# Block sums of the Strassen-like feed-forward: two of four by accumulating transfers, signs moved to the tokens' sums, output chunks placed at bank copies

## The chip, the cores and the metric

The kernel runs on one core of a Trainium2 chip, which has five engines that run side by side: TensorE (PE, matrix products), VectorE (DVE), ScalarE (ACT), GpSimd (POOL) and SyncE (SP, which here only issues transfers). The metric is the device time of one execution in microseconds (us). Lower is better.

## The reference

One decoder layer on 256 tokens of width 1024: a mixing stage with two branches, attention over 256 memory tokens, and a gated feed-forward, each added to the residual stream, and a final norm. The change touches the feed-forward alone:

```python
hn = rmsnorm(h, norm_ffn_g[l])
gu = hn @ w_ffn_in[l]                       # (256, 1024) @ (1024, 5632)
h = h + (jax.nn.silu(gu[..., :FFN_HIDDEN]) * gu[..., FFN_HIDDEN:]) @ w_ffn_out[l]   # FFN_HIDDEN = 2816
return rmsnorm(h, final_norm_g)
```

All inputs and outputs are float32.

## The kernel before

**Products in three.** Each float32 operand is split into a high part (`hi`, rounded to the matmul's float32r) and a low part (`lo`, what is left), and each product is made of three matmuls: hi·hi, hi·lo and lo·hi. For a weight block of 128 x 2048, `halve` makes the high part on ScalarE (L1098) and the low part on VectorE (L1099). Every block of weights passes through these two lines once. Three `hi`/`lo` buffers rotate, with a fourth pair, `px`, for every fourth unit.

**Units of the feed-forward.** The hidden width of 2816 falls into 11 chunks of 256. The plan `FFN_PLAN` is a list of 42 units that TensorE runs in the order written:

- `("I", o, kh)`: the product of the tokens with one half (512 rows) of the input weights of chunk `o`, gate and value columns side by side. Ten of these units, for chunks 0, 1, 4, 7 and 10, are computed directly.
- `("P", q, name)`: chunks 2 and 3, 5 and 6, 8 and 9 are computed in pairs, three double groups `q` = 2, 5, 8. The two halves of the tokens (`t`), the two halves of the depth and the two chunks form a 2 x 2 by 2 x 2 block product, made with seven products instead of eight, in the order P1, P2, P6, P7, P5, P3, P4. Each is 12 matmuls of 512 columns.
- `("O", o)`: output chunk `o`, the product of the hidden values of chunk `o` with its output weights, accumulated in four PSUM banks (`acc`).

**Block sums.** `load_blocks(q)` loads four blocks of the group, named "22", "12", "11" and "21", from SyncE's queue (L1113). The seven products need four sums of these blocks, each made in place by `both` as two VectorE instructions of 128 x 1024 (L1106): one at the load (onto "12"), one for P6 (onto "11"), one for P5 (onto "12" again), one for P4 (onto "21"). The corresponding sums of the tokens (`token_sums`, L1241) are made once and split into `SS`.

**Banks.** P1, P6, P5 and P3 accumulate one after the other in bank A; P2 has bank B, P7 and P4 bank F. What bank A holds after P1, P6 and P5 is copied away by ScalarE (`keep`, L1275) before the next of them may write there. `whole` (L1280) adds a kept copy to another bank. When a half of the hidden values of a chunk is complete, `gate` makes the Silu on ScalarE (`fg`, L1205) and the product on VectorE (`fu`, L1208).

**Turns.** Before output chunk `o` can run, its hidden values are transposed on TensorE (`turn_hid`, L1210, four transposes into `hidT`) and split into `hids` (L310 on ScalarE, L311 on VectorE). `TURNS` says ahead of which unit this is done, and `LOADS` ahead of which unit the blocks of a group are asked for. Weights are prepared three units ahead (`prep_u(n + 3)`).

**Who sets the order.** TensorE's order is the program's. ScalarE, VectorE, GpSimd and SyncE are put in order by the framework's scheduler, by priority in program order and by what it estimates to be ready.

**A path not taken.** The kernel has an option `BY_DMA`, off, in which two of the four sums are made by accumulating transfers from GpSimd's queue, with a negated copy on ScalarE ahead of each (`less`, L1119).

Of the kernel before, what the change touches and what calls it, by code (L numbers as in the profile page):

```python
# [13 lines left out]
AF = mybir.ActivationFunctionType  # L14
ALU = mybir.AluOpType
# [58 lines left out]
def ffn_plan():  # L74
    def seven(q, **after):
        out = []
        for p in SEVEN:
            out.append(("P", q, p))
            out += [("O", o) for o in after.get(p, ())]
        return out  # L80

    def two(j):
        return [("I", j, 0), ("I", j, 1)]

    out = two(0) + two(1)
    out += seven(2, P2=[0], P5=[1]) + two(4)
    out += seven(5, P2=[2], P7=[3], P5=[4]) + two(7)
    out += seven(8, P2=[5], P7=[6], P5=[7])
    out += two(10) + [("O", 8)]
    return out + [("O", 9), ("O", 10)]  # L90

FFN_PLAN = ffn_plan()
BY_DMA = False
LOADS = {0: (2,), 10: (5,), 22: (8,)}
TURNS = {4: (0,), 8: (1,), 15: (2,), 18: (3,), 20: (4,), 27: (5,), 30: (6,), 32: (7,), 38: (8, 9)}


def lay(ws):
# [45 lines left out]
def build(tc, A, out):  # L144
    nc = tc.nc
    V, SC, G, PE, SY = nc.vector, nc.scalar, nc.gpsimd, nc.tensor, nc.sync
    with ExitStack() as ctx:
# [11 lines left out]
        def big(tag, name, shape=(128, 8, 256), dt=F32):  # L159
            return bp.tile(list(shape), dt, name=name, tag=tag)  # L160
# [69 lines left out]
        def nxt(lead=LEAD):  # L230
            i = at[0]
            at[0] += 1
            while made[0] <= min(i + lead, len(ORDER) - 1):
                run(prep())
            return ready.pop(i)
# [31 lines left out]
        def by_k(w, k):  # L267
            return tuple(t.rearrange("p (k c) -> p k c", k=k) for t in w)
# [265 lines left out]
        for i in range(9):  # L534
            if i < 8:
                c, k = i // 4, i % 4
# [4 lines left out]
            if i > 0:  # L541
                c, k = (i - 1) // 4, (i - 1) % 4
                for t in range(2):
                    PE.matmul(pss[c][t], Xh[:, k, t * 128:(t + 1) * 128], ws[c][1][:, k], start=False, stop=False)
        w = by_k(nxt(), 4)
# [15 lines left out]
        w = by_k(nxt(), 4)  # L561
# [483 lines left out]
        for c in range(4):  # L1045
            gemm_f(H1, ev_sum(qxh, qxl, c))
            g = scores(c)
# [36 lines left out]
        where = {u: i for i, u in enumerate(ORDER)}  # L1084
        px = big("P1", "px", (128, 4096), F32R)
        made_u, pair, blk = [0], {}, {}

        def halve(raw, n):
            if n % 4 == 3:
                hi, lo = px[:, 0:2048], px[:, 2048:4096]  # L1090
            else:
                hi = wh.tile([128, 2048], F32R, name="hi", tag="hi")
                lo = wl.tile([128, 2048], F32R, name="lo", tag="lo")
            pieces = 2 if n < 2 else 1
            w = 2048 // pieces
            for c in range(pieces):
                a = slice(c * w, (c + 1) * w)
                SC.activation(hi[:, a], raw[:, a], AF.Copy)  # L1098
                V.tensor_tensor(lo[:, a], raw[:, a], hi[:, a].bitcast(F32), op=ALU.subtract)  # L1099
            return hi, lo  # L1100


        def both(out, x, y, op):
            for i in range(2):
                a = slice(1024 * i, 1024 * i + 1024)
                V.tensor_tensor(out[:, a], x[:, a], y[:, a], op=op)  # L1106

        def load_blocks(q):
            blk.clear()
            for key, tag, c in (("22", "B12", (q + 1, 1)), ("12", "B6", (q + 1, 0)),  # L1110
                                ("11", "B10", (q, 0)), ("21", "B11", (q, 1))):
                blk[key] = big(tag, "b" + key, (128, 2048))
                SY.dma_start(blk[key], A["w"][where[("I",) + c]])  # L1113
            if BY_DMA:
                less(blk["12"], blk["12"], (q + 1, 1))
            else:
                both(blk["12"], blk["22"], blk["12"], ALU.subtract)

        def less(out, x, c):  # L1119
            SC.activation(out, x, AF.Copy, scale=-1.0)  # L1120
            G.dma_start(out, A["w"][where[("I",) + c]], accum_op=ALU.add)

        def block(q, name):
            if name == "P7" and BY_DMA:
                less(blk["21"], blk["11"], (q, 1))
            if name == "P6":
                both(blk["11"], blk["12"], blk["11"], ALU.add)
            elif name == "P5":
                both(blk["12"], blk["22"], blk["11"], ALU.subtract)
            elif name == "P4" and not BY_DMA:  # L1130
                both(blk["21"], blk["21"], blk["11"], ALU.subtract)
            return blk[{"P1": "11", "P2": "21", "P6": "11", "P7": "12", "P5": "12", "P3": "22", "P4": "21"}[name]]

        units = FFN_PLAN
# [50 lines left out]
        for t in range(2):  # L1185
            for c in range(2):
                ps = mm.tile([128, 512], F32, name="pso", tag="mm")
# [11 lines left out]
        X2 = (h2h, h2l)  # L1199
        hid, acc, psi, hm = {}, {}, {}, {}  # L1200

        def gate(o, t):
            ps = psi.pop((o, t))
            g = t2b("fg", (128, 256))
            SC.activation(g, ps[:, 0:256], AF.Silu)  # L1205
            if o not in hm:
                hm[o] = t2("fu", (128, 2, 256))
            V.tensor_tensor(hm[o][:, t], ps[:, 256:512], g, op=ALU.mult)  # L1208

        def turn_hid(o):  # L1210
            bk = mm.tile([128, 2, 256], F32, name="hidT", tag="mm")
            u = hm.pop(o)
            for t in range(2):
                for j in range(2):
                    PE.transpose(bk[:, j, t * 128:(t + 1) * 128], u[:, t, j * 128:(j + 1) * 128], ident)
            hd = hids[o // 2 % 2][:, o % 2]
            split(bk, hd[:, 0], hd[:, 1])
            hid[o] = hd

        def out_part(o, w, t, c, home=None, u=0, v=512):  # L1220
            if home is None and (t, c) not in acc:
                acc[t, c] = bank("acc")
            ps = home or acc[t, c]
            ts, cs = slice(t * 128, (t + 1) * 128), slice(c * 512 + u, c * 512 + v)
            for k in range(2):
                hh, hl = hid[o][:, 0, k], hid[o][:, 1, k]
                mm3t(ps, hh[:, ts], hl[:, ts], w[0][:, k, cs], w[1][:, k, cs],
                     (o == 0 or home is not None) and k == 0, k == 1 and o >= NF // 2 - (2 if t and c else 1))
# [12 lines left out]
        def token_sums():  # L1241
            a11, a12, a21, a22 = (h2g[t, c] for t in range(2) for c in range(2))

            def put(i, g):
                SC.activation(SS[:, 0, i], g, AF.Copy)
                V.tensor_tensor(SS[:, 1, i], g, SS[:, 0, i].bitcast(F32), op=ALU.subtract)

            V.tensor_tensor(a22, a21, a22, op=ALU.add)
            s2 = t2("s2", (128, 4, 128))
            V.tensor_tensor(s2, a22, a11, op=ALU.subtract)  # L1250
            put(1, s2)
            V.tensor_tensor(a21, a11, a21, op=ALU.subtract)
            put(2, a21)
            put(0, a22)
            V.tensor_tensor(a12, a12, s2, op=ALU.subtract)
            put(3, a12)

        def tokens(name):
# [13 lines left out]
        bank_of, kept = {}, {}  # L1272
# [4 lines left out]

        def whole(q, t, ps, key):
            c = t2("fc")
            V.tensor_tensor(c, ps, kept.pop(key), op=ALU.add)  # L1280
            psi[q, t] = c
            gate(q, t)

        def ffn_product(n):
            _, q, name = units[n]
            w = by_k(pair[n], 4)
            key = {"P1": "A", "P6": "A", "P5": "A", "P3": "A", "P2": "B", "P7": "F", "P4": "F"}[name]
            first = name in ("P1", "P2", "P7")
            if first:
                bank_of[key] = mm.tile([128, 512], F32, name="pq" + key, tag="mm")  # L1290
            ps = bank_of[key]
            product(ps, name, w, first)
            if name == "P1":
                keep("1", ps, t2("f1"))
            elif name == "P2":
                whole(q, 0, ps, "1")
            elif name == "P6":
                keep("2", ps, gf[:, 1024:1536])
            elif name == "P5":
                keep("4", ps, gf[:, 1536:2048])  # L1300
                whole(q + 1, 1, bank_of["F"], "4")
            elif name == "P3":
                psi[q + 1, 0] = ps
                gate(q + 1, 0)
            elif name == "P4":
                whole(q, 1, ps, "2")

        def ffn_out(n):
            w = by_k(pair[n], 2)
            for t in range(2):  # L1310
                for c in range(2):
                    out_part(units[n][1], w, t, c)


        prep_u(3)
# [11 lines left out]
        for n in range(4, len(units) - 2):  # L1327
            for q in LOADS.get(n, ()):
                load_blocks(q)
            prep_u(n + 3)  # L1330
            for o in TURNS.get(n, ()):
                turn_hid(o)
# [11 lines left out]
        n = NF // 2 - 1  # L1344
# [38 lines left out]
        with tc.manual_schedule(engines={E.Activation, E.DVE, E.Pool, E.SP}):  # L1383
# [24 lines left out]
            for i in range(2):  # L1408
                a = slice(512 + 256 * i, 768 + 256 * i)
# [46 lines left out]
```

## Time and profile before

| | |
|---|---|
| time, median of 3 runs | 620.22 us (620.06 to 620.54) |
| profiled execution | 619.96 us, span 618.2 us |
| granted TensorE clock | 0.999 |
| the feed-forward's products | from about 430 us to 610 us of the span |
| transfers, feed-forward blocks | `b<-w` 12 of 1024 KB, median 5.9 us from issue to landing |

All times of rows are microseconds from the start of the span. A row of the order of time has its start, its duration, the engine, the line, the operation, what it writes and reads, and in square brackets the engine's idle time just before it and what ended that. Adjacent rows of an engine overlap a little, since an instruction's start and end are in the pipeline of the next one. In a table by stage, each engine has its busy time in the stretch and the number of its instructions. A group's row ends with its busy time, the mean of one in ns, and the idle time of its engine just before these instructions.

### The profile page before, as it was taken

How to read it: one execution, taken by the hardware profiler on the slowest of the kernel's cores; microseconds unless marked ns; L12 is line 12 of the kernel's file. 1: busy time of each engine (PE TensorE's matmuls, PEld its weight loads, DVE VectorE, ACT ScalarE, POOL GpSimd, SP SyncE). 2: the span in 40 equal slices, each digit the busy share in tenths (PEclk: the TensorE clock that was granted, in tenths of full speed). 3: DMA queues.
4: the chain of work that ended last, by engine and by line, in shares of the span. 5: the costliest groups of instructions: out<-in, count | busy, mean ns of one | idle time of the engine just before them, and what ended most of it. 6: DMA issues, size and time to landing. Idle time of an engine off the chain costs nothing.

```text
span 618.2 us, 8376 instructions
## 1 busy us (share of the span) xinstructions
PE 607.5 (98%) x3117; PEld 506.7 (82%) x3117; DVE 460.0 (74%) x714; ACT 355.2 (57%) x545; POOL 256.5 (41%) x227
## 2 busy tenths in 40 slices
PE   8999999999999999999999999999998999999995
PEld 7888888888877877778888888888886888888884
DVE  7589988979766875747855456655799897997743
ACT  7785554334376756736456566746567556565432
POOL 3888744556544464355876876720000000000003
PEclk9999999999999999999999999999999999999999
DMA  8753553334543333644454554463815718613311
GB/s 346 289 204 150 205 200 140 137 136 140 189 150 136 137 137 124 208 181 149 191 205 152 193 200 156 163 227 142 335 68 193 283 69 325 218 68 137 141 64 68
DMA packets 16888, 107.50 MB, mean 174 GB/s; under 512 B 2000, under 2 KB 2640, under 8 KB 4560
## 3 DMA queue, kind: packets, MB, share of 16 engines
q1 hardware_dynamic: 16128, 106.14, 46.5%
q10 hardware_dynamic: 720, 0.84, 0.4%
q8 instruction: 24, 0.39, 0.2%
q14 instruction: 16, 0.13, 0.1%
HBM read 105.92 MB, written 1.05 MB: 173 GB/s over the span
## 4 chain that ended last, share of the span: by engine, by line
PE 89%; DVE 7%; issue 1%; ACT 1%; DMA 1%; POOL 0%; POOLq 0%; DVEq 0%; ACTq 0%
PE pst L263 13%; PE pst L265 13%; PE pst L264 13%; PE psf L284 7%; PE pqA L1269 4%; PE psf L285 4%; PE acc L265 3%; PE acc L263 3%; PE acc L264 3%; DVE lo L1099 2%; PE psi L263 2%; PE psi L265 2%; PE pqF L1269 2%; PE psi L264 2%; PE lp L638 2%; DVE b L1106 1%
## 5 line engine op out<-in xcount | busy, mean ns | idle before, releaser
L223 POOL TENSOR_TENSOR lo<-raw,hi 128x448 fp32r<-128x448 f32 x106 | 161.7, 1540 | 110.6 <-ACT hi L219 107.8
L219 ACT ACTIVATE hi<-raw 128x1024 fp32r<-128x1024 f32 (+1 forms) x128 | 128.7, 1028 | 93.7 <-PE pst L265 58.1
L223 DVE TENSOR_TENSOR lo<-raw,hi 128x576 fp32r<-128x576 f32 (+2 forms) x128 | 131.1, 1031 | 57.2 <-ACT hi L219 54.2
L263 PE MATMUL pst<-hi,XX 128*128 128x512 f32 x224 | 90.5, 404 | 0.0
L265 PE MATMUL pst<-hi,XX 128*128 128x512 f32 x224 | 87.4, 390 | 0.0
L264 PE MATMUL pst<-lo,XX 128*128 128x512 f32 x224 | 87.4, 390 | 0.0
L1374 POOL TENSOR_TENSOR hg<-H,gf 128x512 f32<-128x512 f32 x3 | 3.8, 1290 | 172.1 <-DVE H L1366 172.1
L1099 DVE TENSOR_TENSOR lo<-raw,hi 128x2048 fp32r<-128x2048 f32 (+1 forms) x21 | 43.7, 2086 | 12.2 <-ACT hi L1098 12.1
L265 PEld LDWEIGHTS pst<-hi,XX 128*128 128x128 f32 x224 | 42.1, 188 | 9.0
L263 PEld LDWEIGHTS pst<-hi,XX 128*128 128x128 f32 x224 | 42.1, 188 | 8.8 <-issue 0.7
L264 PEld LDWEIGHTS pst<-lo,XX 128*128 128x128 f32 x224 | 42.2, 188 | 7.8
L1098 ACT ACTIVATE hi<-raw 128x2048 fp32r<-128x2048 f32 (+1 forms) x21 | 36.6, 1750 | 16.4 <-issue 5.6
L1099 DVE TENSOR_TENSOR lo<-b,hi 128x2048 fp32r<-128x2048 f32 x13 | 29.8, 2289 | 8.0 <-ACT hi L1098 8.0
L265 PE MATMUL acc<-hi,hids 128*128 128x512 f32 x78 | 30.7, 393 | 1.7 <-DVE hids L311 1.7
L1098 ACT ACTIVATE hi<-b 128x2048 fp32r<-128x2048 f32 x13 | 24.9, 1914 | 12.1 <-PE acc L265 6.2
L263 PE MATMUL acc<-hi,hids 128*128 128x512 f32 x78 | 30.7, 393 | 0.0
L264 PE MATMUL acc<-lo,hids 128*128 128x512 f32 x78 | 30.4, 390 | 0.0
L1106 DVE TENSOR_TENSOR b<-b,b 128x1024 f32<-128x1024 f32 x24 | 28.5, 1219 | 0.0
L263 PE MATMUL psi<-hi,H 128*128 128x512 f32 x72 | 28.1, 391 | 0.0
L265 PE MATMUL psi<-hi,H 128*128 128x512 f32 x72 | 28.1, 390 | 0.0
L264 PE MATMUL psi<-lo,H 128*128 128x512 f32 x72 | 28.0, 389 | 0.0
L284 PE MATMUL psf<-H,hi 128*128 128x512 f32 x64 | 22.8, 400 | 0.0
(402 smaller groups left out, 1485.1 us busy)
## 6 DMA issues: line engine op xcount, KB each, us to landing
raw<-w SPq DMA_DIRECT2D x82, 1024.0 KB, 4.8
b<-w SPq DMA_DIRECT2D x12, 1024.0 KB, 5.9
raw<-w SPq DMA_DIRECT2D x4, 512.0 KB, 6.3
raw<-w SPq DMA_DIRECT2D x4, 256.0 KB, 4.0
H<-xtok SPq DMA_DIRECT2D x1, 1024.0 KB, 9.5
mraw<-mT SPq DMA_DIRECT2D x1, 1024.0 KB, 4.8
xraw<-xT SPq DMA_DIRECT2D x1, 512.0 KB, 6.4
gf<-gfin SPq DMA_DIRECT2D x1, 512.0 KB, 3.6
```

What stands on the lines that cost most here:

```text
L219: SC.activation(hi[:, a], raw[:, a], AF.Copy)
L223: eng.tensor_tensor(lo[:, b], raw[:, b], hi[:, b].bitcast(F32), op=ALU.subtract)
L263: PE.matmul(ps, xh, h, start=first, stop=False)
L264: PE.matmul(ps, xh, l, start=False, stop=False)
L265: PE.matmul(ps, xl, h, start=False, stop=last)
L284: PE.matmul(ps, w[0][:, k, a], X2[:, :, k], start=k == 0, stop=False)
L285: PE.matmul(ps[:, 0], w[1][:, k, a], X2[:, 0, k], start=False, stop=k == 7)
L638: PE.matmul(ps[:, j], KS[:, a0 + j], QQ[:, a0 + j], start=True, stop=True)
L1098: SC.activation(hi[:, a], raw[:, a], AF.Copy)
L1099: V.tensor_tensor(lo[:, a], raw[:, a], hi[:, a].bitcast(F32), op=ALU.subtract)
L1106: V.tensor_tensor(out[:, a], x[:, a], y[:, a], op=op)
L1269: PE.matmul(ps, x[k], z[:, k], start=first and k == 0 and i == 0, stop=k == 3 and i == 2, skip_group_check=not first)
```

## The change

Two of the four block sums of each double group are taken from VectorE: the one at the load becomes a transfer from memory that adds onto block "12", and the one for P4 becomes a transfer inside the core's memory that adds block "11" onto block "21". Both are issued by GpSimd. A transfer can only add, so the block product is written with other signs: the two chunks of a group trade places (`q` and `q + 1`), the signs of the tokens' sums, of P3's gate and of the sum that uses P5's copy change, and the subtractions of blocks that are made by transfer become additions.

Beside it, three smaller things. The high part of every unit is made in two ScalarE instructions of 128 x 1024 (before, only for the first two units), while the low part stays one instruction. In the first double group output chunk 0 moves from behind P2 to behind P7. The turns move to earlier units: those of chunks 2, 5 and 8 now stand right behind P4, ahead of the next direct unit. `MIDWAY` is empty and does nothing.

```diff
-    out = two(0) + two(1)
-    out += seven(2, P2=[0], P5=[1]) + two(4)
+    out = two(0) + two(1) + seven(2, P7=[0], P5=[1]) + two(4)
...
-BY_DMA = False
+BY_DMA = (2, 5, 8)
 LOADS = {0: (2,), 10: (5,), 22: (8,)}
-TURNS = {4: (0,), 8: (1,), 15: (2,), 18: (3,), 20: (4,), 27: (5,), 30: (6,), 32: (7,), 38: (8, 9)}
+TURNS = {4: (0,), 6: (1,), 13: (2,), 16: (3,), 18: (4,), 25: (5,), 28: (6,), 30: (7,), 37: (8,), 38: (9,)}
...
+            for c in range(2):
+                a = slice(c * 1024, (c + 1) * 1024)
+                SC.activation(hi[:, a], raw[:, a], AF.Copy)
             pieces = 2 if n < 2 else 1
             w = 2048 // pieces
             for c in range(pieces):
                 a = slice(c * w, (c + 1) * w)
-                SC.activation(hi[:, a], raw[:, a], AF.Copy)
                 V.tensor_tensor(lo[:, a], raw[:, a], hi[:, a].bitcast(F32), op=ALU.subtract)
...
-            for key, tag, c in (("22", "B12", (q + 1, 1)), ("12", "B6", (q + 1, 0)),
-                                ("11", "B10", (q, 0)), ("21", "B11", (q, 1))):
+            for key, tag, c in (("22", "B12", (q, 1)), ("12", "B6", (q, 0)),
+                                ("11", "B10", (q + 1, 0)), ("21", "B11", (q + 1, 1))):
...
-            if BY_DMA:
-                less(blk["12"], blk["12"], (q + 1, 1))
+            if q in BY_DMA:
+                G.dma_start(blk["12"], A["w"][where["I", q, 1]], accum_op=ALU.add)
             else:
-                both(blk["12"], blk["22"], blk["12"], ALU.subtract)
+                both(blk["12"], blk["22"], blk["12"], ALU.add)
...
             if name == "P6":
                 both(blk["11"], blk["12"], blk["11"], ALU.add)
+            elif name == "P7" and q in BY_DMA:
+                G.dma_start(blk["21"], blk["11"], accum_op=ALU.add)
             elif name == "P5":
-                both(blk["12"], blk["22"], blk["11"], ALU.subtract)
-            elif name == "P4" and not BY_DMA:
-                both(blk["21"], blk["21"], blk["11"], ALU.subtract)
+                both(blk["12"], blk["11"], blk["22"], ALU.subtract)
+            elif name == "P4" and q not in BY_DMA:
+                both(blk["21"], blk["21"], blk["11"], ALU.add)
...
-        def gate(o, t):
+        def gate(o, t, sign=1.0):
...
-            SC.activation(g, ps[:, 0:256], AF.Silu)
+            SC.activation(g, ps[:, 0:256], AF.Silu, scale=sign)
...
+            if sign < 0:
+                V.scalar_tensor_tensor(hm[o][:, t], ps[:, 256:512], sign, g, op0=ALU.mult, op1=ALU.mult)
...
-            V.tensor_tensor(a22, a21, a22, op=ALU.add)
+            V.tensor_tensor(a22, a22, a21, op=ALU.subtract)
             s2 = t2("s2", (128, 4, 128))
-            V.tensor_tensor(s2, a22, a11, op=ALU.subtract)
+            V.scalar_tensor_tensor(s2, a22, -1.0, a11, op0=ALU.mult, op1=ALU.subtract)
...
-            V.tensor_tensor(a12, a12, s2, op=ALU.subtract)
+            V.scalar_tensor_tensor(a12, s2, -1.0, a12, op0=ALU.mult, op1=ALU.subtract)
...
             elif name == "P2":
-                whole(q, 0, ps, "1")
+                whole(q + 1, 0, ps, "1")
...
             elif name == "P5":
                 keep("4", ps, gf[:, 1536:2048])
-                whole(q + 1, 1, bank_of["F"], "4")
+                whole(q, 1, bank_of["F"], "4")
             elif name == "P3":
-                psi[q + 1, 0] = ps
-                gate(q + 1, 0)
+                psi[q, 0] = ps
+                gate(q, 0, -1.0)
             elif name == "P4":
-                whole(q, 1, ps, "2")
+                whole(q + 1, 1, ps, "2")
```

More of the change, by code (lines that the diff above doesn't have):

```diff
@@ L92 @@
 FFN_PLAN = ffn_plan()
-BY_DMA = False
+BY_DMA = (2, 5, 8)
 LOADS = {0: (2,), 10: (5,), 22: (8,)}
-TURNS = {4: (0,), 8: (1,), 15: (2,), 18: (3,), 20: (4,), 27: (5,), 30: (6,), 32: (7,), 38: (8, 9)}
+TURNS = {4: (0,), 6: (1,), 13: (2,), 16: (3,), 18: (4,), 25: (5,), 28: (6,), 30: (7,), 37: (8,), 38: (9,)}
+MIDWAY = {}
 def lay(ws):
@@ L1109, in load_blocks @@
             blk.clear()
-            for key, tag, c in (("22", "B12", (q + 1, 1)), ("12", "B6", (q + 1, 0)),
-                                ("11", "B10", (q, 0)), ("21", "B11", (q, 1))):
+            for key, tag, c in (("22", "B12", (q, 1)), ("12", "B6", (q, 0)),
+                                ("11", "B10", (q + 1, 0)), ("21", "B11", (q + 1, 1))):
                 blk[key] = big(tag, "b" + key, (128, 2048))
                 SY.dma_start(blk[key], A["w"][where[("I",) + c]])
-            if BY_DMA:
-                less(blk["12"], blk["12"], (q + 1, 1))
-            else:
-                both(blk["12"], blk["22"], blk["12"], ALU.subtract)
-        def less(out, x, c):
-            SC.activation(out, x, AF.Copy, scale=-1.0)
-            G.dma_start(out, A["w"][where[("I",) + c]], accum_op=ALU.add)
+            if q in BY_DMA:
+                G.dma_start(blk["12"], A["w"][where["I", q, 1]], accum_op=ALU.add)
+            else:
+                both(blk["12"], blk["22"], blk["12"], ALU.add)
         def block(q, name):
-            if name == "P7" and BY_DMA:
-                less(blk["21"], blk["11"], (q, 1))
             if name == "P6":
                 both(blk["11"], blk["12"], blk["11"], ALU.add)
+            elif name == "P7" and q in BY_DMA:
+                G.dma_start(blk["21"], blk["11"], accum_op=ALU.add)
             elif name == "P5":
-                both(blk["12"], blk["22"], blk["11"], ALU.subtract)
-            elif name == "P4" and not BY_DMA:
-                both(blk["21"], blk["21"], blk["11"], ALU.subtract)
+                both(blk["12"], blk["11"], blk["22"], ALU.subtract)
+            elif name == "P4" and q not in BY_DMA:
+                both(blk["21"], blk["21"], blk["11"], ALU.add)
             return blk[{"P1": "11", "P2": "21", "P6": "11", "P7": "12", "P5": "12", "P3": "22", "P4": "21"}[name]]
@@ L1200, in build @@
         hid, acc, psi, hm = {}, {}, {}, {}
-        def gate(o, t):
+        def gate(o, t, sign=1.0):
             ps = psi.pop((o, t))
             g = t2b("fg", (128, 256))
-            SC.activation(g, ps[:, 0:256], AF.Silu)
+            SC.activation(g, ps[:, 0:256], AF.Silu, scale=sign)
             if o not in hm:
                 hm[o] = t2("fu", (128, 2, 256))
-            V.tensor_tensor(hm[o][:, t], ps[:, 256:512], g, op=ALU.mult)
+            if sign < 0:
+                V.scalar_tensor_tensor(hm[o][:, t], ps[:, 256:512], sign, g, op0=ALU.mult, op1=ALU.mult)
+            else:
+                V.tensor_tensor(hm[o][:, t], ps[:, 256:512], g, op=ALU.mult)
         def turn_hid(o):
@@ L1279, in whole @@
             c = t2("fc")
-            V.tensor_tensor(c, ps, kept.pop(key), op=ALU.add)
+            if key == "4":
+                V.scalar_tensor_tensor(c, ps, -1.0, kept.pop(key), op0=ALU.mult, op1=ALU.subtract)
+            else:
+                V.tensor_tensor(c, ps, kept.pop(key), op=ALU.add)
             psi[q, t] = c
@@ L1312, in ffn_out @@
                     out_part(units[n][1], w, t, c)
+                if t == 0:
+                    for o in MIDWAY.get(n, ()):
+                        turn_hid(o)
         prep_u(3)
```

## The prediction

> **What bounds the kernel now.** I read the page's engine rows first, then the busy times by stage over the feed-forward part, where every edit of the diff lies, then TensorE's waits there.
>
> ```profile
> PE 607.5 (98%) x3117; PEld 506.7 (82%) x3117; DVE 460.0 (74%) x714; ACT 355.2 (57%) x545; POOL 256.5 (41%) x227
> ...
> core 0: us, PE busy (x) PEld busy (x) DVE busy (x) ACT busy (x) POOL busy (x), PEclk, DMA share, GB/s
> 438.00:484.00 46.00, 43.62 (x198) 35.25 (x197) 43.13 (x40) 28.79 (x29) 0.00 (x0) 1.00 0.50 198
> 484.00:538.00 54.00, 54.00 (x246) 44.72 (x245) 49.88 (x39) 32.47 (x29) 0.00 (x0) 1.00 0.58 218
> 538.00:594.00 56.00, 56.00 (x258) 46.46 (x257) 44.37 (x35) 31.38 (x29) 0.00 (x0) 1.00 0.31 114
> ```
>
> TensorE (PE) is busy in all of the second and third double group (54.00 of 54.00, 56.00 of 56.00) at full clock. No matmul is added or taken away, so nothing can be won there. The first double group is different: 43.62 of 46.00, with VectorE (DVE) at 43.13 of 46.00. The waits name the missing 2.38 us:
>
> ```profile
> engine line waited for: us in total, times, longest us
> PE acc L265 <- DVE hids L311: 1.7, 1, 1.7
> PE pqA L1269 <- ACT gf L1275: 0.7, 1, 0.7
> ...
> 471.60 0.51 PE L1269 MATMUL pqA<-hi,SS 128*128 128x512 f32 x1 [0.69 <-ACT gf L1275]
> ...
> 474.70 0.39 PE L264 MATMUL acc<-lo,hids 128*128 128x512 f32 x1
> 476.76 0.50 PE L265 MATMUL acc<-hi,hids 128*128 128x512 f32 x1 [1.67 <-DVE hids L311]
> ```
>
> The first stall is P5, the second is output chunk 1, which needs the split of its turned hidden values (L311). Both are prices of a late queue, which VectorE's order of time shows:
>
> ```profile
> 454.14 2.28 DVE L1099 TENSOR_TENSOR lo<-raw,hi 128x2048 fp32r<-128x2048 f32 x1
> 456.34 0.42 DVE L1208 TENSOR_TENSOR fu<-psi,fg 128x256 f32<-128x256 f32 x1
> 456.67 2.35 DVE L1106 TENSOR_TENSOR b<-b,b 128x1024 f32<-128x1024 f32 x2
> 458.94 0.69 DVE L311 TENSOR_TENSOR hids<-hidT,hids 128x512 fp32r<-128x512 f32 x1
> 459.54 2.28 DVE L1099 TENSOR_TENSOR lo<-b,hi 128x2048 fp32r<-128x2048 f32 x1
> 461.74 2.29 DVE L1099 TENSOR_TENSOR px<-b,px 128x2048 fp32r<-128x2048 f32 x1
> ...
> 466.00 3.50 DVE L1106 TENSOR_TENSOR b<-b,b 128x1024 f32<-128x1024 f32 x3
> 469.41 2.29 DVE L1099 TENSOR_TENSOR lo<-b,hi 128x2048 fp32r<-128x2048 f32 x1
> ...
> 476.02 0.69 DVE L311 TENSOR_TENSOR hids<-hidT,hids 128x512 fp32r<-128x512 f32 x1
> ```
>
> There are no gaps: P5's low part ends at 471.70, beside P5's start at 471.60, and the split for chunk 1 ends at 476.71, 0.05 before TensorE resumes.
>
> **The change part by part.** *Two sums of four leave VectorE.*
>
> ```profile
> L1106 DVE TENSOR_TENSOR b<-b,b 128x1024 f32<-128x1024 f32 x24 | 28.5, 1219 | 0.0
> ```
>
> Each sum is two of these; 12 of 24 go, 14.6 us of VectorE in all and 4.9 us in each double group. In the second and third group they cover no TensorE wait and bring 0. In the first, 4.9 us leave a queue that made TensorE wait 0.69 + 1.67 = 2.36 us.
>
> *Signs.* Eight sums, gates and kept products become three-operand instructions of the same shapes, or carry a scale in the Silu; I take 0, since they have the same elements and are no more in number.
>
> *The high parts go in two halves on ScalarE.*
>
> ```profile
> L1098 ACT ACTIVATE hi<-raw 128x2048 fp32r<-128x2048 f32 x1 | 1.9, 1913 | 0.0
> L1098 ACT ACTIVATE hi<-raw 128x1024 fp32r<-128x1024 f32 x1 | 1.0, 1044 | 0.0
> ```
>
> 2 x 1044 - 1913 = 175 ns more for each of 40 units, 7 us of an engine that is busy 32.47 of 54 us: 0 on the path, with 0.2 us less margin for the low part behind each. A gate can now slip in after 1.04 instead of 1.91 us.
>
> *Order.* In the first group chunk 0 moves from behind P2 to behind P7. The copy of bank A that P5 waits for is then covered by chunk 0, and chunk 1's values are turned at unit 6 instead of 8, so that P6, P7, chunk 0 and P5 lie before their use. P6 is now needed earlier:
>
> ```profile
> 459.05 0.39 PE L263 MATMUL acc<-hi,hids 128*128 128x512 f32 x1
> ...
> 459.68 0.50 PE L265 MATMUL acc<-hi,hids 128*128 128x512 f32 x1
> ...
> 464.81 2.89 PE L1269 MATMUL pqA<-px,SS 128*128 128x512 f32 x12
> ...
> 509.74 0.44 PE hidT L1215 x4
> ```
>
> After the change it starts at 459.05 plus the four transposes of a turn (0.44 us, last row), so at 459.5 instead of 464.81. Its low part ended at 464.03 (row of 461.74). Ahead of it go away the first sum (2 x 1.13 in the queue), and behind it move chunk 0's low part (2.2) and the split for chunk 0 (0.6): 464.03 - 2.27 - 2.2 - 0.6 = 459.0; if P7's low part (2.2) also falls behind it, as the program's order has it, 456.8. So it is ready 0.5 to 2.7 us before it is due; I take no stall, and 0.5 us as its price if another low part stays ahead (459.0 plus 0.2 from the halves is the near end).
>
> *Accumulating transfers.* GpSimd issues them; its queue is empty here (0.00 busy): the power at 435.12 below is its last work before, ahead of the transfer's wait that ends at 436.7, so nothing is behind that wait. Each group has one from memory onto block 12, and one from block 11 onto block 21. For the first, GpSimd waits for the landing of 12, and P6's sum on VectorE waits for it; behind that sum stand gates and low parts, and TensorE waits for those. The block's own load:
>
> ```profile
> 430.67 0.33 SPq L1113 DMA_DIRECT2D b<-w  x1
> ...
> DMA to landing us min/median/max: 6.0/6.0/6.0
> ...
> DMA to landing us min/median/max: 5.3/7.0/10.1
> ...
> 435.12 0.56 POOL L1164 TENSOR_TENSOR r<-v,nhalf 128x1 f32<-128x1 f32 x1 [13.93 <-DVE v L1162]
> ...
> 469.56 2.49 SPq L1113 DMA_DIRECT2D b<-w  x2
> ...
> 510.18 2.77 PE pqA L1269 x12
> ```
>
> It lands at 436.7 (first landing row; the second is that of the group's four loads). Backward from P6 at 459.5: low part 2.29, second half of the high part 1.04, the sum 2.27, together 5.6, so the accumulate has until 453.9, 17.2 us. No accumulate is in this trace. The low bound of its price is the fastest of the four loads, 5.3 us; an estimate of the high bound is three passes (read, read, write) of the slowest, 3 x 10.1 = 30.3 us. I take 10.1, a load of the same size in the same full queue: landing at 446.8, 7 us of room, cost 0. The Trainium skill, page "Collectives: The Full Stack", section "The bandwidth ceiling: the fold count and why AG ≠ RS ≠ AR", says that an add in the transfer engines runs at half a copy's rate, not because of the add but since it reads two sources; no run shows it yet. By it the price would be 20.2 us, landing at 456.9, and the sum below would lose 3.0 us. The second accumulate is issued after P6's sum (about 454) and is needed for P4. Between lie P6, P7, P5 and P3 at 2.72 and two chunks at about 5.5 (459.68 to 464.81 and the half microsecond before), so P4 is due at 459.5 + 21.9 = 481.4, its block 1.9 + 2.3 earlier, at 477.2: 23 us, cost 0 even at 20. In the second group the loads are issued from 469.56 and P6 starts at 510.18 (last rows), so there the room is more than twice that of the first. SyncE's queue keeps its number of loads; three of the accumulates add 3 MB of memory reads at a DMA share of 0.58 or less.
>
> *The turns go right behind P4 (chunks 2, 5, 8).* The gate of P3 now completes the hidden values that are turned next, with only P4's 12 matmuls between. P3, its gate and the next start on TensorE in two groups of before:
>
> ```profile
> 482.06 2.72 PE pqA L1269 x12
> 484.78 2.72 PE pqF L1269 x12
> ...
> 486.31 2.35 DVE L1106 TENSOR_TENSOR b<-b,b 128x1024 f32<-128x1024 f32 x2
> 488.58 0.42 DVE L1208 TENSOR_TENSOR fu<-pqA,fg 128x256 f32<-128x256 f32 x1
> ...
> 529.74 2.72 PE pqA L1269 x12
> ...
> 531.78 2.29 DVE L1099 TENSOR_TENSOR lo<-raw,hi 128x2048 fp32r<-128x2048 f32 x1
> 534.00 0.42 DVE L1208 TENSOR_TENSOR fu<-pqA,fg 128x256 f32<-128x256 f32 x1
> ```
>
> In the second group the gate ends 534.42 - 532.46 = 1.96 us after P3; the cover is 2.72, so 0.76 are left, about 0.55 with the halves. In the first it ended 489.00 - 484.78 = 4.22 after P3, but 2.27 of that is the next group's first sum (486.31), which the change removes: 1.95. I take 0; the bounds are 0 and 4.22 - 2.72 = 1.50 us a group.
>
> **The sum.** The profiled execution took 619.96 us (span 618.2), 0.26 below the median of 620.22. 619.96 - 0.69 - 1.67 = 617.60, and the two matmuls that restart after the waits (0.51 and 0.50 instead of 0.39) give back about 0.2: **617.4 us**, 2.8 below the median. What this kernel's measurement can tell from no change is 0.2%, 1.24 us.
>
> **The rivals.** *A: the gates come too late for the turns (slower).* It acts at units 13, 25 and 37 and decides where the gate behind P3 ends more than 2.72 us after P3. At the first group's old row it costs 1.50 three times: 617.4 + 4.5 = 621.9. Two of the three old groups speak against it (1.96 in the second); for it, that one more low part of 2.2 ahead of the gate is enough. Over 2.8 + 1.24 = 4.0 us, 1.35 a group, make it slower.
>
> *B: the accumulate is late for P6 in the first group.* At 20.2 us it gives back 3.0: 620.4, no change. At 30.3 it lands at 467.0, 13.1 late: 630.5. Against it stand 17.2 us of room; for it, a full queue, since four loads and two others are under way.
>
> *C: the relief is partly lost.* P6 brought forward by 5.3 us meets a VectorE that is still nearly full (43.13 - 4.9 of 46), or one turn waits: 1 to 2.5 us of new stalls, 618.4 to 619.9, most of it within 0.2%.
>
> *D: nothing of the transfers' promise shows*, since the order alone ends both waits: the same 617.4, told apart only by VectorE's queue.
>
> **How the numbers follow.** The forecast, with D, has 0.60; C 0.17 (0.03 of it still faster, 0.14 same); A 0.12 (0.02 same, 0.10 slower); B 0.11 (0.02 same, 0.09 slower). So faster 0.63, same 0.18, slower 0.19. The range begins at 616.8: the forecast less 0.3 for a wait at chunk 0's split (the matmul two after 459.05 starts at 459.68, where two steps of 2.72/12 take 0.45) that moves away too and 0.3 for the run's spread (620.06 to 620.54 around the median). It ends at 622.1, A's price with 0.2 on it; left out are B's far end and the tails.
>
> **What would show it.** Right: no TensorE wait at P5 or at chunk 1 in the first group, 12 rows of block sums instead of 24, VectorE about 4.9 us less busy up to the first group's end, and GpSimd's transfers landing before 453.9. Wrong: a TensorE wait at `hidT` behind P4 (A), at `pqA` for P6 with the block sum waiting on a transfer (B), or at P6 with VectorE full (C).

## The result and the profile after

The changed kernel takes 618.63 us (median of 9 runs, 617.89 to 619.70), the kernel before on the same chip 620.22 (619.87 to 621.00). The ratio is 0.9975, 95% interval 0.9965 to 0.9985: a gain of 0.25%, some 1.6 us, where 2.8 were forecast. The profiled execution took 617.99 us with a span of 616.1.

The engine row, the same three stages of the feed-forward as before, and TensorE's waits from 430 to 606 us (a header with no row below it):

```profile
PE 607.1 (99%) x3117; PEld 506.8 (82%) x3117; DVE 446.7 (72%) x702; ACT 358.5 (58%) x585; POOL 262.3 (43%) x233
...
438.00:484.00 46.00, 46.00 (x213) 38.10 (x212) 41.36 (x39) 32.10 (x42) 2.85 (x3) 1.00 0.80 254
484.00:538.00 54.00, 54.00 (x247) 44.65 (x246) 43.22 (x35) 31.35 (x40) 1.77 (x2) 1.00 0.85 272
538.00:594.00 56.00, 56.00 (x256) 46.34 (x255) 41.28 (x33) 32.12 (x41) 0.86 (x1) 1.00 0.42 132
...
engine line waited for: us in total, times, longest us
```

TensorE is busy in all 46.00 us of the first stage, where 2.38 were missing; both old waits are gone and no new one has come. VectorE has 12 block-sum rows instead of 24, and 41.36 us of work instead of 43.13 in that stage. That is only 1.8 us less because the kernel is further on at the stretch's end: counted from 438 us up to the end of the gate behind P3 (489.00 before, 484.06 after), VectorE works 48.0 us before and 41.4 after, with ten and four rows of block sums. Of the six rows that went, two are the next group's first sum.

What is new are the transfers. The first rows are the queues (packets, MB, share of the span that their packets took on the 16 transfer engines), then the issues (count, size, median from issue to landing), then GpSimd's order of time in the first group, and the landing of its first accumulate (accumulating transfer) alone:

```profile
q1 hardware_dynamic: 16128, 106.14, 46.5%
q0 software_dynamic: 864, 6.29, 5.3%
...
b<-w SPq DMA_DIRECT2D x12, 1024.0 KB, 6.7
b<-w POOLq DMA_DIRECT2D x3, 1024.0 KB, 12.9
b<-b POOLq DMA_DIRECT2D x3, 1024.0 KB, 8.3
...
440.40 1.11 POOL L1117 DMA_DIRECT2D b<-w  x1 [6.61 <-PE h2T L1175]
455.84 0.87 POOL L1125 DMA_DIRECT2D b<-b  x1 [14.33 <-DVE fu L1210]
...
DMA to landing us min/median/max: 12.2/12.2/12.2
```

The first accumulate lands at 440.4 + 12.2 = 452.6. ScalarE's row that waits for it (P7's high part, whose weights are block 12 itself), VectorE's order there, and the first matmul of P6 that needs its low part:

```profile
452.69 1.06 ACT L1096 ACTIVATE px<-b 128x1024 fp32r<-128x1024 f32 x1 [2.09 <-DMA b<-w]
...
450.73 2.28 DVE L1101 TENSOR_TENSOR lo<-b,hi 128x2048 fp32r<-128x2048 f32 x1
452.93 2.35 DVE L1108 TENSOR_TENSOR b<-b,b 128x1024 f32<-128x1024 f32 x2
455.20 0.41 DVE L1210 TENSOR_TENSOR fu<-psi,fg 128x256 f32<-128x256 f32 x1
455.53 2.28 DVE L1101 TENSOR_TENSOR px<-b,px 128x2048 fp32r<-128x2048 f32 x1
457.73 2.28 DVE L1101 TENSOR_TENSOR lo<-b,hi 128x2048 fp32r<-128x2048 f32 x1
459.94 0.68 DVE L311 TENSOR_TENSOR hids<-hidT,hids 128x512 fp32r<-128x512 f32 x1
...
460.10 0.47 PE L1271 MATMUL pqA<-lo,SS 128*128 128x512 f32 x1
```

The transfer is there 0.3 us before the block sum that needs it (452.93). P7's low part (`px`, 455.53) goes ahead of P6's (457.73), which ends at 460.01, as TensorE comes to it. No wait is left, but no room either.

### The profile page after: what moved, and what is told of

Its sections match the earlier page's. It is cut to its first block, busy times and chain, and to the rows that moved or that the text cites. A ratio compares the mean times of both kernels' runs of the same rounds, so it can differ in the third digit from the quotient of the medians.

```text
span 616.1 us, 8425 instructions
## 1 busy us (share of the span) xinstructions
PE 607.1 (99%) x3117; PEld 506.8 (82%) x3117; DVE 446.7 (72%) x702; ACT 358.5 (58%) x585; POOL 262.3 (43%) x233
## 3 DMA queue, kind: packets, MB, share of 16 engines
q1 hardware_dynamic: 16128, 106.14, 46.5%
q0 software_dynamic: 864, 6.29, 5.3%
## 4 chain that ended last, share of the span: by engine, by line
PE 95%; DVE 1%; ACT 1%; DMA 1%; issue 1%; POOL 0%; POOLq 0%; DVEq 0%; ACTq 0%
PE pst L263 13%; PE pst L265 13%; PE pst L264 13%; PE psf L284 7%; PE pqA L1271 5%; PE psf L285 4%; PE acc L265 3%; PE acc L263 3%; PE acc L264 3%; PE psi L263 3%; PE psi L265 3%; PE psi L264 3%; PE pqF L1271 3%; PE lp L638 2%; PE pqB L1271 1%; PE psg L539 1%
## 5 line engine op out<-in xcount | busy, mean ns | idle before, releaser
L1096 ACT ACTIVATE hi<-raw 128x1024 fp32r<-128x1024 f32 x38 | 38.2, 1052 | 15.4 <-DMA raw<-w 5.6
L1096 ACT ACTIVATE hi<-b 128x1024 fp32r<-128x1024 f32 x26 | 26.3, 1052 | 16.6 <-DMA b<-w 7.7
L1125 POOL DMA_DIRECT2D b<-b x3 | 2.6, 873 | 54.6 <-ACT hi L1096 21.6
L1117 POOL DMA_DIRECT2D b<-w x3 | 2.9, 955 | 47.9 <-DVE lo L1101 20.7
## 6 DMA issues: line engine op xcount, KB each, us to landing
b<-w POOLq DMA_DIRECT2D x3, 1024.0 KB, 12.9
```

## The experiments

The runs were made in three sets, each on a chip of its own with the kernel before beside it: 620.87 us for the kernel before in the set of the changed kernel again, the order without transfers, and block 12 first and last; 620.42 in the set of the late groups, the transfers without the order, the whole high parts and the old turns; 620.60 in the set of the other four. The ratios are those on record, which are not exactly quotients of the medians (they differ by up to 0.0008).

The profiles give a second measure, free of what happens ahead of the feed-forward: the time from its first matmul (the first that writes `psi`) to the end of the span. It is 187.7 us before and 185.3, 185.3 and 185.6 in the changed kernel's three profiles. The table has it for the other kernels, to within 0.1 us.

| kernel | us |
|---|---|
| order without transfers | 188.8 |
| transfers in the second and third group alone | 186.8 |
| transfers without the new order | 186.9 |
| block 12 first (two profiles) | 185.1, 185.7 |
| block 12 last | 186.2 |
| high parts whole, and with block 12 first as well | 187.1, 187.3 |
| halves in the first group alone | 186.4 |
| old turns from chunk 2 on | 185.5 |

**The changed kernel again.** No edit.

> The changed kernel once more, on the chip of the next three. Theory J (the first accumulate lands just in time, 452.61 against the block sum's 452.93 in the first profile, and in some runs too late): median about 618.6 again with a spread of over 1 us, and a profile of one of its longer runs shows a TensorE wait at P6 of 0.5 to 1.5 us and the accumulate landing after 453. Theory K (the spread is not of this place): a longer run has no TensorE wait in the first double group.

Measured: 618.39 us (617.80 to 619.24), ratio 0.9962 (0.9948 to 0.9976). Its profile fell on a short run (617.80) and has no wait in the feed-forward, so it tells nothing between the expectation's two theories, J and K.

**Order without transfers.**

```diff
-BY_DMA = (2, 5, 8)
+BY_DMA = ()
```

> All four block sums back on VectorE; signs, order, turns and halved high parts as in the changed kernel. Theory S (the transfers' relief of VectorE carries the gain): VectorE has 4.9 us more up to the end of the first group, so TensorE waits about 2 us in all at P6, P5 or chunk 1, and the time is 619.8 to 620.6. Theory D (the order alone ends both waits): 618 to 618.7, no wait of TensorE.

Measured: 622.67 us, ratio 1.0029 (1.0019 to 1.0039): 1.8 us slower than before the change. TensorE's waits, all that are listed in the feed-forward, then VectorE at the turn of chunk 2:

```profile
PE hidT L1217 <- DVE fu L1208: 2.4, 1, 2.4
PE pqA L1271 <- DVE lo L1101: 1.3, 1, 1.3
...
484.03 2.29 DVE L1101 TENSOR_TENSOR lo<-raw,hi 128x2048 fp32r<-128x2048 f32 x1 [1.45 <-ACT hi L1096]
486.24 2.35 DVE L1108 TENSOR_TENSOR b<-b,b 128x1024 f32<-128x1024 f32 x2
488.51 0.42 DVE L1208 SCALAR_TENSOR_TENSOR fu<-pqA,fg 128x256 f32<-128x256 f32 x1
```

Both old waits, at P5 and at chunk 1, are gone with the order alone, but two new ones have come. P6 is asked for 5 us earlier of a full VectorE (1.3), and the gate behind P3 stands behind the next group's first sum (486.24), so the turn behind P4 waits 2.4 us. That is rival A's mechanism, and the transfer of that sum is what keeps it away in the changed kernel. Theory D falls, since it allowed for no new wait. S is right that the transfers carry the gain, but its range (619.8 to 620.6) is missed by 2 us: it had the wait at P6 and not the one at the turn.

**Transfers in the second and third group alone.**

```diff
-BY_DMA = (2, 5, 8)
+BY_DMA = (5, 8)
```

> The first double group's sums go back to VectorE, the second and third keep their transfers. Theory S (the gain is the relief in the first group): TensorE waits 1.3 to 1.6 us at P6 as with all sums on VectorE, but not at the turn at unit 13, since the second group's first sum is still a transfer; time 619.8 to 620.6. Rival (the transfers count in the later groups alone): 618.4, no wait at P6.

Measured: 619.67 us, ratio 0.9980 (0.9969 to 0.9991).

```profile
PE pqA L1271 <- DVE lo L1101: 1.3, 1, 1.3
...
PE hidT L1217 <- DVE fu L1208: 0.2, 1, 0.2
```

The wait at P6 stays, the one at the turn is down from 2.4 to 0.2. So the first group's transfers are worth the 1.3 us at P6, and the second group's first transfer the 2.2 at the turn. That is as theory S had it, and its time (619.8 to 620.6) is missed by a tenth.

**Transfers without the new order.** The plan and the turns of before:

```diff
-    out = two(0) + two(1) + seven(2, P7=[0], P5=[1]) + two(4)
+    out = two(0) + two(1) + seven(2, P2=[0], P5=[1]) + two(4)
-TURNS = {4: (0,), 6: (1,), 13: (2,), ...
+TURNS = {4: (0,), 8: (1,), 15: (2,), ...
```

> Transfers, signs and halved high parts, but chunk 0 behind P2 and the turns at their old units. Theory S (VectorE's late queue made both old waits): both go, 618.0 to 618.7. Rival (the order made them, the queue only their length): 0.5 to 1.7 us of waits stay at P5 and chunk 1, time 619 to 620.

Measured: 619.82 us, ratio 0.9991 (0.9980 to 1.0001). The profile fell on the longest run (621.96), but its feed-forward starts at 433.2 instead of 430.8 us, so most of that excess lies ahead of it.

```profile
PE acc L265 <- DVE hids L311: 1.8, 1, 1.8
...
475.50 2.28 DVE L1101 TENSOR_TENSOR px<-b,px 128x2048 fp32r<-128x2048 f32 x1
477.70 0.68 DVE L311 TENSOR_TENSOR hids<-hidT,hids 128x512 fp32r<-128x512 f32 x1
```

The wait at P5 is gone, the one at chunk 1 is as long as ever: its split stands behind three low parts on VectorE whatever was taken away earlier in the queue. Theory S falls here: the new order is what removes this wait, as the rival said. Whether the early turn of chunk 1 alone does it, or chunk 0's new place too, was not separated.

**Block 12 loaded first, and last.** Block 12 and block 11 trade buffers, or block 12 goes to the end of the list:

```diff
-for key, tag, c in (("22", "B12", (q, 1)), ("12", "B6", (q, 0)), ("11", "B10", ...), ("21", "B11", ...)):
+for key, tag, c in (("12", "B10", (q, 0)), ("22", "B12", (q, 1)), ("11", "B6", ...), ("21", "B11", ...)):   # first
+for key, tag, c in (("22", "B12", (q, 1)), ("11", "B10", ...), ("21", "B11", ...), ("12", "B6", (q, 0))):   # last
```

> Blocks 12 and 11 trade buffers, so that block 12 is loaded first and its accumulate starts some 5 us earlier in the first group (landing near 447.5 instead of 452.6). Theory J: with 5 us of room the longer runs go away, median 617.9 to 618.1, spread under 0.8 us. Theory K: 618.6 with the same spread of 1.8 us.

> Block 12 is loaded last of the four, so its accumulate starts about 2.5 us later. Theory J: the accumulate lands at 454.5 to 455.5, P6's sum waits about 2 us for it on VectorE, TensorE waits 1.5 to 2.5 us at P6, time 620 to 621. Theory K (the landing has room that the rows don't show): 618.6 and no TensorE wait.

Measured: first 617.78 us, ratio 0.9955 (0.9941 to 0.9968); last 618.66, ratio 0.9971 (0.9958 to 0.9985). GpSimd's issue of the first accumulate in the two, then the block sum and TensorE's wait where it comes last:

```profile
434.60 1.11 POOL L1117 DMA_DIRECT2D b<-w  x1 [1.01 <-DMA b<-w]
...
443.29 1.11 POOL L1117 DMA_DIRECT2D b<-w  x1 [9.70 <-DMA b<-w]
...
453.41 2.36 DVE L1108 TENSOR_TENSOR b<-b,b 128x1024 f32<-128x1024 f32 x2 [0.59 <-DMA b<-w]
...
PE pqA L1271 <- DVE lo L1101: 0.5, 1, 0.5
```

Issued 2.9 us later than in the changed kernel, the transfer lands after 10.0 us instead of 12.2 and is 0.6 us late, not 2 (fewer other loads under way by then may be why; that was not tried); VectorE waits 0.59 and TensorE 0.5 for it. So the place has no room, as J says, and a late landing goes through to TensorE; the size that J expected was too large, and the median can't be told from the changed kernel's. Nor does an early landing make room. With block 12 first the transfer lands at 434.6 + 13.9 = 448.5, and P6's low part still ends at 459.82, just before the matmul that needs it (459.90): the order on VectorE, with P7's low part ahead of P6's, leaves no more than a tenth there either.

**Again side by side.** Block 12 first and the changed kernel once more, with no other edit:

> The kernel with block 12 loaded first once more, beside the changed kernel on one chip. Theory J (the landing in the first group has no room in the changed kernel): 0.3 to 0.8 us less than the changed kernel's median. Theory K (the spread is from ahead of the feed-forward): the same within 0.3 us.

> The changed kernel a third time, for the comparison with the kernel that loads block 12 first: 618.4 to 618.7.

Measured: 618.52 us (617.59 to 619.14) and 618.59 (617.73 to 619.83), ratios 0.9968 (0.9955 to 0.9980) and 0.9969 (0.9960 to 0.9979). The 0.6 us of the first comparison are not there again, as theory K expected: that loading block 12 first is faster is not shown. In this profile of it (execution 618.52) a wait stands in the second group. The rows are TensorE's wait; VectorE's order before it; ScalarE's; the landing of a plain load of that group, issued at 477.38; and the landing of the load at the same place (479.47) in the order without transfers:

```profile
PE pqB L1271 <- DVE fu L1210: 0.4, 1, 0.4
...
490.43 1.23 DVE L1108 TENSOR_TENSOR b<-b,b 128x1024 f32<-128x1024 f32 x1 [3.17 <-DMA b<-w]
492.76 0.42 DVE L1210 TENSOR_TENSOR fu<-fc,fg 128x256 f32<-128x256 f32 x1 [1.10 <-ACT fg L1204]
...
499.24 0.75 DVE L1210 TENSOR_TENSOR fu<-psi,fg 128x256 f32<-128x256 f32 x2
...
490.42 2.01 ACT L1096 ACTIVATE hi<-b 128x1024 fp32r<-128x1024 f32 x2 [6.45 <-DMA b<-w]
492.33 0.40 ACT L1204 ACTIVATE fg<-fc 128x256 f32<-128x256 f32 x1
...
DMA to landing us min/median/max: 12.9/12.9/12.9
...
DMA to landing us min/median/max: 7.4/7.4/7.4
```

VectorE stands 3.17 us before half of a block sum, because the second group's accumulate (477.70 + 12.6) has not landed. That is not what holds up P2, though: the half sum ends at 491.66, and VectorE then stands another 1.10 us for a gate's `fg`. That `fg` stands on ScalarE behind the high part of block 21, which waits 6.45 us for its plain load. The load was issued 0.3 us before the accumulate and took 12.9 us, where it took 7.4 with no accumulate beside it; TensorE's chain of waits goes back to it, through ScalarE and VectorE to chunk 4's gates at 499.24, which P2 waits for. The changed kernel has the same pattern (12.4 us of load, 6.07 of idle on ScalarE, 3.50 on VectorE), with no wait of TensorE.

The third profile of the changed kernel (execution 618.76) has no listed wait in the feed-forward, but this one earlier, which the first profile has not:

```profile
PE psg L539 <- ACT hi L219: 0.6, 1, 0.6
```

It is 0.77 longer than the first (617.99). Half of that lies ahead of the feed-forward (its first matmul is at 431.3 instead of 430.8), as K says. The other half lies in it, where no wait is listed, and its cause stays open. J's late landing was seen in no profile of the changed kernel.

**The high parts whole again.**

```diff
-            for c in range(2):
-                a = slice(c * 1024, (c + 1) * 1024)
-                SC.activation(hi[:, a], raw[:, a], AF.Copy)
             pieces = 2 if n < 2 else 1
+            for c in range(pieces):
+                a = slice(c * 2048 // pieces, (c + 1) * 2048 // pieces)
+                SC.activation(hi[:, a], raw[:, a], AF.Copy)
```

> High parts in one ScalarE instruction again from the third unit on. Theory: the halves lie beside other work, 618.1 to 618.7, no new wait. Rival (P6's weights have no margin, and a whole high part can only start when both halves of the sum are there): a wait of 0.5 to 1.2 us at P6, 619 to 619.8.

> High parts whole as before, and block 12 loaded first, so that the first accumulate lands 4 us earlier. Theory (the late transfer makes the wait at P6, the whole high parts make the one at P5): the 0.3 us at P6 go, about 1 us stays at P5, time 619.2 to 619.9. Rival (both waits come from the late transfer): 617.8 to 618.3.

Measured: 620.32 us, ratio 0.9998 (0.9988 to 1.0009); with block 12 loaded first as well 620.17, ratio 0.9995 (0.9986 to 1.0003). The whole gain is gone, and the earlier transfer does not bring it back. TensorE's waits (the same row in both kernels), then ScalarE and VectorE ahead of P5 with whole high parts, then the same in the changed kernel:

```profile
PE pqA L1271 <- DVE lo L1101: 1.2, 2, 0.9
...
466.41 1.92 ACT L1097 ACTIVATE px<-b 128x2048 fp32r<-128x2048 f32 x1 [1.71 <-PE pqF L1271]
468.23 1.90 ACT L1097 ACTIVATE hi<-b 128x2048 fp32r<-128x2048 f32 x1
468.36 2.29 DVE L1101 TENSOR_TENSOR px<-b,px 128x2048 fp32r<-128x2048 f32 x1 [0.98 <-ACT px L1097]
470.57 2.28 DVE L1101 TENSOR_TENSOR lo<-b,hi 128x2048 fp32r<-128x2048 f32 x1
```

```profile
464.29 1.06 ACT L1096 ACTIVATE px<-b 128x1024 fp32r<-128x1024 f32 x1 [0.36 <-PE pqF L1271]
465.26 1.04 ACT L1096 ACTIVATE hi<-b 128x1024 fp32r<-128x1024 f32 x1
...
467.15 1.04 ACT L1096 ACTIVATE hi<-b 128x1024 fp32r<-128x1024 f32 x1
...
468.23 2.29 DVE L1101 TENSOR_TENSOR lo<-b,hi 128x2048 fp32r<-128x2048 f32 x1 [1.61 <-ACT hi L1096]
```

P5 waits 0.9 us and P6 0.3. Whole, block 22's high part (`px`, for P3) runs ahead of P5's, so its low part does too, and P5's low part ends at 472.85. In halves the scheduler lays the blocks' halves between each other: P5's second half ends at 468.2 and its low part is the first on VectorE, ending 470.5. At P6 it is the order too, now on ScalarE. With whole high parts and block 12 first:

```profile
453.78 0.39 ACT L1204 ACTIVATE fg<-psi 128x256 f32<-128x256 f32 x1 [3.25 <-PE psi L265]
454.06 1.91 ACT L1097 ACTIVATE px<-b 128x2048 fp32r<-128x2048 f32 x1
```

The transfer landed at 435.03 + 13.7 = 448.7, but P7's high part (`px`) stands behind a gate for which ScalarE idles 3.25 us; in halves its first half goes ahead of that gate (452.69 in the changed kernel). What the halves change is the order of the queue; they take no work away. Of the expectations the first run's rival came nearest, though its one wait is two and the time lies above its range; that the wait at P6 would go with an earlier transfer was wrong, as was the rival that both would.

**Halves in the first group alone.** `cuts = 2 if n < 2 or 4 <= n <= 12 else 1`

> High parts in halves only for units 4 to 12, the first double group (and the first two units, as before). Theory (VectorE is full there alone, so only there the order and start of the low parts matter): 618.0 to 618.8, no wait of TensorE. Rival (the halves act in the later groups): 619.5 or more.

Measured: 619.45 us, ratio 0.9985 (0.9976 to 0.9994).

```profile
PE pqB L1272 <- DVE fu L1211: 0.8, 1, 0.8
```

No wait of the first group is listed, but P2 of the second waits 0.8 us for a gate, at the same place as above and again behind a plain load of 12.6 us. Somewhat less than half of what whole high parts lose comes back with halves in the first group, and the rest shows at the second group's P2. The theory had only the first group; the time lies 0.05 below the rival's range.

**The old turns from chunk 2 on.**

```diff
-TURNS = {4: (0,), 6: (1,), 13: (2,), 16: (3,), 18: (4,), 25: (5,), 28: (6,), 30: (7,), 37: (8,), 38: (9,)}
+TURNS = {4: (0,), 6: (1,), 15: (2,), 18: (3,), 20: (4,), 27: (5,), 30: (6,), 32: (7,), 38: (8, 9)}
```

> The turns from chunk 2 on are at their old units; chunk 1's stays at unit 6. Theory: the cover of 2.72 us behind P3 is enough, so the early turns neither cost nor bring anything: 618.1 to 618.7 and no wait in either. Rival A (the gates are too close to the turns in the longer runs): 0.5 to 1 us less than the changed kernel, 617.5.

Measured: 618.69 us, ratio 0.9965 (0.9952 to 0.9978). No difference that can be seen: the turns right behind P4 neither cost nor bring anything, as expected.

## Why the prediction was right, and where it was not

*The sum.* The direction and the range held, and the waits named are the ones that went. That the feed-forward came out near the sum is partly luck. 2.36 us plus 0.2 of restarts were forecast. From the feed-forward's first matmul to the last that writes `acc` TensorE gained more, 3.2 us (430.47 to 609.75 before, 430.85 to 606.96 after), part of it at chunk 0's split, which the prediction put into its range. Behind that matmul the span lasts 9.2 us instead of 8.4. The prediction had no term there; this stretch is 8.4 us in both profiles without transfers and 8.7 to 9.3 in the twelve with them, and what lengthens it was not found. Together that makes 2.4 us. The part ahead became 0.4 longer. The rest is in what was compared: 617.4 was counted from a profiled execution 0.26 below its median and then set against the median, while the median of the changed kernel lies 0.64 above its profiled execution. So 2.8 were promised by medians and 1.6 came.

*Both waits, and what ends them.* They go, but by more than one cause. Rival D is right that the order alone ends both, and wrong that nothing else comes: order alone is 1.8 us slower than before, where D had 2.8 faster. Without the order the wait at chunk 1 stays; without the halves one at P5 is back. Only together do they work. Each was left out in turn; none was tried alone on the kernel before.

*The halves at 0.* This is the step that failed most: they are worth 1.8 us (ratios 0.9998 and 0.9969; 187.1 and 185.3 us in the profiles), all of the gain by the medians and three quarters of it by the profiles. The relief of VectorE and the order, to which the sum gave the whole 2.36, bring little without them, so that the total came out near is luck in this too: the sum gave the credit to two parts of the change where it took three. The working counted ScalarE's time and asked what covered 175 ns; it did not ask in which order two blocks' parts would come out of ScalarE onto VectorE.

*The accumulate.* The load taken for block 12's was another block's: by the semaphores that their readers wait for, the scheduler had put them in the order 11, 22, 12, 21. Block 12's load, issued at 431.41, lands after 8.3 us at 439.7, and GpSimd issues at 440.40, not at 436.7 (434.60 with block 12 loaded first). And the price was 12.2 us, not 10.1: landing 452.6 instead of 446.8, 0.3 us before its use where 7 of room were forecast. The cost of 0 was right by luck. In the second group the room forecast for the accumulate itself was there: it lands at 490.3, P6 starts at 507.6. What the prediction left out is what the transfers do to the loads beside them. It counted 3 MB more of reads at a DMA share of 0.58 or less; the share rose to 0.80 and 0.85 in the first two stages (0.52 and 0.57 with the order alone). The three plain loads issued just ahead of and behind the second group's accumulate took 12.4, 12.0 and 10.7 us; at the same place in the order without transfers they took 7.4, 7.0 and 6.9. It is such a load that the waits at the second group's P2 go back to.

*The half rate.* The queue rows give 5.3 / 6.29 = 0.84% of the span per MB for the accumulates and 46.5 / 106.14 = 0.44 for plain transfers, a ratio of 1.9. That agrees with the half rate that the Trainium skill's page "Collectives: The Full Stack" states in "The bandwidth ceiling: the fold count and why AG ≠ RS ≠ AR" for the add of a collective. By the landing the doubling of 10.1 was too dear: 20.2 against 12.2 measured, in a queue with other loads.

*The turns behind P4.* Right at 0: the gate ends at 484.06 before the turn at 484.44 in the first group, and the old turns change nothing. With the next group's sum on VectorE, as in the order without transfers, rival A happens, at 2.4 us where 1.5 was its price.

*P6 brought forward.* Forecast ready 0.5 to 2.7 us before its start at 459.5; it was ready at 460.01, with P6's first matmul, which needs the high part alone, at 459.78 and the next at 460.10. P7's low part did not fall behind it, so the near end of the forecast was the one to take, and that was 0.8 us too early. C's place was right; in the changed kernel its price is nothing that a wait shows, and 1.3 us where the first group's sums stay on VectorE.

## What to carry to other kernels

When a full engine is relieved, read its queue by order and not by load: which low part stands ahead of which decides what is late, and cutting an instruction in two on the engine before it can change that order by more than the instruction costs. A transfer in place of an instruction takes the work away, but somebody now waits for a landing, and the plain transfers beside it land later: ask which loads run at the same time, who waits for them and what stands behind that one in its queue, and not only when the result is due. Edits that each end a wait may be worth nothing or less without the others: leave each out in turn before naming the one that paid.

## What the runs showed of the hardware

An accumulating transfer of 1 MB inside the core's memory took 7.0 us from issue to landing in the first group, and 8.3 in the median; one from memory took 12.9 in the median, where the median of the plain loads of blocks was 6.7. Three plain loads beside an accumulate took 12.4, 12.0 and 10.7 us, and 7.4, 7.0 and 6.9 at the same place in the kernel that differs from it in having no accumulates. GpSimd was busy 0.86 to 1.11 us for each accumulate. The one at 455.84 was issued while VectorE had two-operand instructions without a gap (450.73 to 460.62), and its 0.87 us is no longer than at other times, so nothing here shows that a busy VectorE holds up the issue. All transfers tried here add; whether a transfer could do anything else to a block, as the change's description denies, no run shows.
